# Filling whole tiles with two neighbouring columns (and no zero fill), another order of skipping, and two queues for the last stores in a sliding-window copy

## Chip, cores, metric

The kernel runs on one core of one Trainium2 chip. The metric is the device time of one execution in microseconds (us). Every ratio to the kernel before uses runs of the same rounds on the same chip. Differences to the changed kernel ("than after") compare medians of different rounds, some on other chips; the kernel before stood at 194.77 to 194.96 us in all of them, so differences of 0.2 us mean nothing.

## The reference

The input `x` is 16 x 64 x 64 x 64 float32 (batch, channels, rows, columns). The output holds each 8 x 8 window at stride 4, so 15 x 15 windows per image.

```python
n_h = (h - window_size) // stride + 1          # 15
n_w = (w - window_size) // stride + 1          # 15
for i in range(n_h):
    for j in range(n_w):
        h_start = i * stride
        w_start = j * stride
        result[:, i, j] = x[:, :, h_start:h_start + window_size, w_start:w_start + window_size].copy()
```

There is no arithmetic. 16.8 MB come in, 59.0 MB go out, and one window of one image (64 x 8 x 8 floats) is a contiguous row of 16 KB of the output.

## The kernel before

The input is loaded whole into a tile `L`. Its partition is (channel half, batch, quarter of the image's rows), so a partition holds 32 channels and 16 image rows. The loads of batch half `y=0` are issued before those of `y=1`.

A window row of the output needs all 64 channels on one partition. ScalarE (`act`) and VectorE (`dve`) therefore gather it into one of four 2 MB tiles `G`. GpSimd then stores the tile with an indirect DMA (a scatter) that sends each partition's 16 KB to the output row named by an index; an index beyond the end makes it skip that row.

```python
# (cut) idx: row of the output for partition p; adding FAR makes the scatter skip the partition
def scatter(g, ix, j, s):
    st = nc.gpsimd.indirect_dma_start(
        out=o_v, out_offset=bass.IndirectOffsetOnAxis(ap=ix[:, 0:1], axis=0),
        in_=g.rearrange("p c r w -> p (c r w)"), in_offset=None,
        element_offset=(s * NW + j) * CFREE,
        bounds_check=B * NWIN - 1, oob_is_err=False)
    free(st)

zero = ipool.tile([P, 1], f32, name="zero")
nc.vector.memset(zero[:, :], 0.0)
for g in G:
    act(out=g.rearrange("p c r w -> p (c r w)"), in_=zero.to_broadcast([P, CFREE]))

def part(y, j):                       # first phase: one batch half, so half a tile
    g = tile_()
    for half in range(CH):
        fill(g, half, half, j, y * QP, QP, (dve, dve) if y and half else (act, dve))
    scatter(g, (idx_y0, idx_y1)[y], j, 0)

def unit(j, s):
    # (cut) s == 0: a "plain" tile, 128 rows, index idx
    # s == 2: a "cross" tile; 16 of its 128 rows do not exist and are skipped:
    turn = int(crossed % 5 in (1, 3))
    crossed += 1
    fill(g, turn, s, j, 0, HP, (act, act))
    fill(g, 1 - turn, s + 1, j, 0, HP, (dve, dve))
    scatter(g, (idx_hi, idx_lo)[turn], j, s)

# (cut) order: 3 part(0, .), then 3 x (part(1, .), plain), then (cross, cross, plain) ...
# last column: two half tiles, each stored by four plain DMAs
for q in range(HQ):
    free(nc.sync.dma_start(out=o_q[q * NSLOT + s, j], in_=g_q[QP + q : QP + q + (B - 1) * HQ + 1 : HQ]))
```

A cross tile with index `idx_hi` skips its rows in the upper 64 partitions ("hi" below); one with `idx_lo` skips them in the lower 64 ("lo"). The zero fill initialises the partitions that a half tile leaves unwritten.

Of the kernel before, what the change touches and what calls it, by code (L numbers as in the profile page):

```python
# [10 lines left out]
def kernel(  # L11
# [7 lines left out]
    nc = tc.nc  # L19
    P = nc.NUM_PARTITIONS  # L20

    B, C, H, W = x.shape
    Bo, NH, NW, Co, WSo, WSo2 = out.shape
    WS = int(window_size)
    ST = int(stride)
    assert Bo == B and Co == C and WSo == WS and WSo2 == WS

    f32 = mybir.dt.float32
    i32 = mybir.dt.int32
    ALU = mybir.AluOpType  # L30
    CH = 2
    HQ = P // (B * CH)
    CL = C // CH
    RB = H // HQ
    NSLOT = RB // ST
    NWIN = NH * NW
    CFREE = C * WS * WS
    HP = P // CH
    YB = 8
    NY = B // YB  # L40
    QP = YB * HQ
# [3 lines left out]
    ipool = ctx.enter_context(tc.tile_pool(name="ipool", bufs=1))  # L45
# [3 lines left out]
    L = lpool.tile([P, CL, RB, W], f32)  # L49
# [12 lines left out]
    def itile(name):  # L62
        return ipool.tile([P, 1], i32, name=name)

    pi, tb, tq, tc_, th, idx, idx_y0, idx_y1, idx_lo, idx_hi = (
        itile(n) for n in ("pi", "tb", "tq", "tc", "th", "idx", "idx_y0", "idx_y1", "idx_lo", "idx_hi")
    )
    FAR = float(2 * B * NWIN)
    nc.gpsimd.iota(pi[:, :], pattern=[[0, 1]], base=0, channel_multiplier=1)  # L69

    def bits(d, shift, mask):
        nc.vector.tensor_scalar(out=d[:, :], in0=pi[:, :], scalar1=shift, scalar2=mask, op0=ALU.logical_shift_right, op1=ALU.bitwise_and)  # L72

    def mul(d, a, m):
        nc.vector.tensor_scalar(out=d[:, :], in0=a[:, :], scalar1=float(m), scalar2=None, op0=ALU.mult)  # L75

    def tt(d, a, b, op):
        nc.vector.tensor_tensor(out=d[:, :], in0=a[:, :], in1=b[:, :], op=op)  # L78
# [8 lines left out]
    tt(idx, tb, th, ALU.add)  # L87

    bits(th, 5, 1)
    mul(th, th, FAR)  # L90
    tt(idx_y0, idx, th, ALU.add)
    nc.vector.tensor_scalar(out=th[:, :], in0=th[:, :], scalar1=-1.0, scalar2=FAR, op0=ALU.mult, op1=ALU.add)
    tt(idx_y1, idx, th, ALU.add)

    nc.vector.tensor_scalar(out=tq[:, :], in0=tq[:, :], scalar1=float(HQ - 1), scalar2=FAR, op0=ALU.is_equal, op1=ALU.mult)
    tt(th, tc_, tq, ALU.mult)
# [17 lines left out]
    NG = 4  # L114
    G = [gpool.tile([P, C, WS, WS], f32, name=f"G{n}") for n in range(NG)]

    o_q = out.rearrange("b i j c r w -> i j b (c r w)")

    def free(st):
        tc.declare_no_dep(st.ins, group="stores", reason="each store writes rows of its own")  # L120
        tc.add_to_no_dep_group("stores", st.ins)

    def scatter(g, ix, j, s):
        st = nc.gpsimd.indirect_dma_start(  # L124
            out=o_v,
            out_offset=bass.IndirectOffsetOnAxis(ap=ix[:, 0:1], axis=0),
            in_=g.rearrange("p c r w -> p (c r w)"),
            in_offset=None,
            element_offset=(s * NW + j) * CFREE,
            bounds_check=B * NWIN - 1,  # L130
            oob_is_err=False,
        )
        free(st)

    def fill(g, half, s, j, lo, n, copies):

        d = slice(half * HP + lo, half * HP + lo + n)
        cols = slice(j * ST, j * ST + WS)
        for ch in (half, 1 - half):
            f = slice(ch * HP + lo, ch * HP + lo + n)  # L140
            cs = slice(ch * CL, (ch + 1) * CL)
            copy = copies[ch != half]
            if s < NSLOT - 1:
                copy(out=g[d, cs, :, :], in_=L[f, :, s * ST : s * ST + WS, cols])  # L144
            else:
                copy(out=g[d, cs, 0:ST, :], in_=L[f, :, s * ST : RB, cols])  # L146
                nc.vector.stream_shuffle(out=g[d, cs, ST:WS, :], in_=L[f, :, 0:ST, cols], mask=nxt)  # L147

    act, dve = nc.scalar.copy, nc.vector.tensor_copy



    EARLY = NG - 1
    zero = ipool.tile([P, 1], f32, name="zero")
    nc.vector.memset(zero[:, :], 0.0)  # L155
    for g in G:
        act(out=g.rearrange("p c r w -> p (c r w)"), in_=zero.to_broadcast([P, CFREE]))  # L157
    at = 0

    def tile_():  # L160
        nonlocal at
        at += 1
        return G[(at - 1) % NG]

    def part(y, j):
        g = tile_()
        for half in range(CH):
            fill(g, half, half, j, y * QP, QP, (dve, dve) if y and half else (act, dve))
        scatter(g, (idx_y0, idx_y1)[y], j, 0)

    crossed = 0

    def unit(j, s):
        nonlocal crossed
        g = tile_()
        if s == 0:
            for half in range(CH):
                fill(g, half, half, j, 0, HP, (act, dve))
            scatter(g, idx, j, s)
        else:  # L180

            turn = int(crossed % 5 in (1, 3))
            crossed += 1
            fill(g, turn, s, j, 0, HP, (act, act))
            fill(g, 1 - turn, s + 1, j, 0, HP, (dve, dve))
            scatter(g, (idx_hi, idx_lo)[turn], j, s)

    for j in range(EARLY):
        part(0, j)
    plain = [(j, 0) for j in range(EARLY, NW - 1)]  # L190
    cross = [(j, 2) for j in range(NW)]
    for j in range(EARLY):
        part(1, j)
        unit(*plain.pop(0))
    while plain:
        for w in cross[:2]:
            unit(*w)
        cross = cross[2:]
        unit(*plain.pop(0))


    j = NW - 1
    tile_()
    for s in range(2):
        g = tile_()
        cols = slice(j * ST, j * ST + WS)
        for y in range(NY):
            d = slice(QP + y * QP, QP + (y + 1) * QP)
            for ch, copy in enumerate((act, dve)):
                f = slice(ch * HP + y * QP, ch * HP + (y + 1) * QP)  # L210
                copy(out=g[d, ch * CL : (ch + 1) * CL, :, :], in_=L[f, :, s * ST : s * ST + WS, cols])  # L211
        g_q = g.rearrange("p c r w -> p (c r w)")
        for q in range(HQ):
            free(nc.sync.dma_start(out=o_q[q * NSLOT + s, j], in_=g_q[QP + q : QP + q + (B - 1) * HQ + 1 : HQ]))


# [33 lines left out]
```

## Time and profile before

| | before |
|---|---|
| median of its first runs | 194.92 us (194.81 to 195.02) |
| span of the profiled run | 192.9 us |
| busy: DVE, ACT, POOL | 57%, 72%, 28% |
| mean DMA rate | 393 GB/s |

The columns of a group are line, engine, operation, output<-input, count, then busy us and mean ns, then idle time before and what ended it.

```profile
DMA packets 11588, 75.81 MB, mean 393 GB/s; under 512 B 3888, under 2 KB 3888, under 8 KB 7984
...
L157 ACT COPY G<-zero 128x4096 f32<-128x4096 f32 x4 | 14.1, 3600 | 0.0
...
L157 ACT ACT_TABLE_LOAD x1 | 1.3, 1283 | 0.7 <-PEq L231 0.7
```

The table load belongs to the first ScalarE copy of the program. Here that is the zero fill, so the load runs at 0.7 us, when nobody waits for ScalarE.

### The profile page before, as it was taken

The numbers are of one execution on the slowest core, as the hardware profiler recorded it, in microseconds if no ns is written. First come the engines' busy times: TensorE is split into PE (matmuls) and PEld (weight loads), VectorE is DVE, ScalarE is ACT, GpSimd is POOL, SyncE is SP. The second block draws the span as 40 slices with busy tenths as digits, with TensorE's granted clock in tenths as the row PEclk, the third lists the DMA queues.
The fourth block names the chain that finished last, engine by engine and source line by source line (L and its number), as shares of the span: only waits on it lengthen the run. The fifth ranks groups of instructions, "written<-read, shape, count | busy, mean of one in ns | idle before, by whom it ended". The sixth has DMA issues, their size and how long they took to land.

```text
span 192.9 us, 487 instructions
## 1 busy us (share of the span) xinstructions
DVE 110.2 (57%) x153; ACT 138.3 (72%) x70; POOL 54.6 (28%) x53
## 2 busy tenths in 40 slices
DVE  5000007700999979876876875874974794723330
ACT  8993008940897879999778777877977797754560
POOL 7402212531166430422214123134043124320000
DMA  2999999999989999999999999999999999999764
GB/s 79 337 404 400 399 401 397 401 401 407 421 357 418 404 423 421 425 421 404 426 425 428 420 411 418 432 435 411 404 435 418 425 431 404 418 432 435 321 292 177
DMA packets 11588, 75.81 MB, mean 393 GB/s; under 512 B 3888, under 2 KB 3888, under 8 KB 7984
## 3 DMA queue, kind: packets, MB, share of 16 engines
q0 software_dynamic: 9472, 66.34, 83.8%
q1 hardware_dynamic: 2112, 9.44, 12.4%
q14 instruction: 4, 0.03, 0.0%
HBM read 16.78 MB, written 69.21 MB: 446 GB/s over the span
## 4 chain that ended last, share of the span: by engine, by line
DMA 73%; DVE 12%; issue 7%; POOL 2%; ACTq 1%; ACT 1%; DVEq 0%; PEldq 0%
DMA out_dram<-G,idx 34%; DMA out_dram<-G,idx_hi 22%; DMA L<-in_x_dram 16%; DVE G L144 9%; POOL L L58 2%; DVE G L146 2%; DVE G L147 2%; ACTq L245 1%; ACT G L211 1%; DVEq L144 0%; POOL pi L69 0%; DVEq L146 0%; PEldq L245 0%; ACTq L211 0%
## 5 line engine op out<-in xcount | busy, mean ns | idle before, releaser
L144 ACT COPY G<-L 64x2048 f32<-64x2048 f32 (+1 forms) x61 | 115.3, 1896 | 40.0 <-issue 20.7
L144 DVE COPY G<-L 64x2048 f32<-64x2048 f32 (+1 forms) x37 | 45.0, 1224 | 41.9 <-DMA L<-in_x_dram 27.1
L147 DVE STREAM_SHUFFLE G<-L 64x1024 f32<-64x1024 f32 x30 | 38.3, 1277 | 0.0
L146 DVE COPY G<-L 64x1024 f32<-64x1024 f32 x30 | 21.6, 720 | 21.5 <-DMA out_dram<-G,idx 16.2
L124 POOL DMA_INDIRECT out_dram<-G,idx_hi x9 | 12.0, 1338 | 34.9 <-DVE G L147 24.5
L58 POOL DMA_DIRECT2D L<-in_x_dram x16 | 11.4, 715 | 23.9 <-DMA L<-in_x_dram 23.4
L124 POOL DMA_INDIRECT out_dram<-G,idx x11 | 12.4, 1126 | 18.6 <-ACT G L144 15.9
L124 POOL DMA_INDIRECT out_dram<-G,idx_lo x6 | 8.9, 1480 | 24.1 <-DVE G L147 17.0
L124 POOL DMA_INDIRECT out_dram<-G,idx_y x6 | 9.6, 1603 | 16.0 <-ACT G L144 8.9
L157 ACT COPY G<-zero 128x4096 f32<-128x4096 f32 x4 | 14.1, 3600 | 0.0
L211 ACT COPY G<-L 32x2048 f32<-32x2048 f32 x4 | 7.6, 1896 | 7.4 <-DMA out_dram<-G,idx 4.9
L211 DVE COPY G<-L 32x2048 f32<-32x2048 f32 x4 | 4.9, 1220 | 10.1 <-DMA out_dram<-G,idx 6.6
L157 ACT ACT_TABLE_LOAD x1 | 1.3, 1283 | 0.7 <-PEq L231 0.7
L155 DVE MEMSET zero<- 128x1 f32 x1 | 0.1, 59 | 0.8 <-PEq L231 0.8
L78 DVE CUSTOM_DVE_ANT_0 idx_y<-idx,th 128x2 uint16<-128x2 uint16 x2 | 0.3, 160 | 0.1
L78 DVE TENSOR_TENSOR th<-tc,tq 128x1 int32<-128x1 int32 x2 | 0.3, 158 | 0.1
L75 DVE TENSOR_SCALAR th<-tc 128x1 int32<-128x1 int32 x2 | 0.3, 154 | 0.0
L69 POOL IOTA pi<- 128x1 int32 x1 | 0.1, 125 | 0.4 <-PEq L245 0.4
L72 DVE TENSOR_SCALAR tb<-pi 128x1 int32<-128x1 int32 x1 | 0.2, 154 | 0.1
L147 DVE LOAD_MASK_SELECT G<-L x30 | 0.2, 6 | 0.0
L78 DVE CUSTOM_DVE_ANT_0 idx_hi<-idx,th 128x2 uint16<-128x2 uint16 x1 | 0.2, 160 | 0.0
L78 DVE CUSTOM_DVE_ANT_0 idx<-tb,th 128x2 uint16<-128x2 uint16 x1 | 0.2, 159 | 0.0
(16 smaller groups left out, 2.2 us busy)
## 6 DMA issues: line engine op xcount, KB each, us to landing
L<-in_x_dram POOLq DMA_DIRECT2D x8, 1024.0 KB, 21.0
L<-in_x_dram SPq DMA_DIRECT2D x8, 896.0 KB
out_dram<-G SPq DMA_DIRECT2D x8, 256.0 KB
L<-in_x_dram POOLq DMA_DIRECT2D x8, 128.0 KB, 21.1
out_dram<-G,idx POOLq DMA_INDIRECT x11, 14.5
out_dram<-G,idx_hi POOLq DMA_INDIRECT x9, 14.1
out_dram<-G,idx_y POOLq DMA_INDIRECT x6, 9.8
out_dram<-G,idx_lo POOLq DMA_INDIRECT x6, 12.9
```

The costliest lines, as they stand in the source:

```text
L58: eng.dma_start(out=L[p0 : p0 + QP - HQ + 1 : HQ, c0:c1, :, :], in_=x_v[ch, y, q, :, c0:c1, :])
L69: nc.gpsimd.iota(pi[:, :], pattern=[[0, 1]], base=0, channel_multiplier=1)
L72: nc.vector.tensor_scalar(out=d[:, :], in0=pi[:, :], scalar1=shift, scalar2=mask, op0=ALU.logical_shift_right, op1=ALU.bitwise_and)
L75: nc.vector.tensor_scalar(out=d[:, :], in0=a[:, :], scalar1=float(m), scalar2=None, op0=ALU.mult)
L78: nc.vector.tensor_tensor(out=d[:, :], in0=a[:, :], in1=b[:, :], op=op)
L124: st = nc.gpsimd.indirect_dma_start(out=o_v, out_offset=bass.IndirectOffsetOnAxis(ap=ix[:, 0:1], axis=0), in_=g.rearrange("p c r w -> p (c ...
L144: copy(out=g[d, cs, :, :], in_=L[f, :, s * ST : s * ST + WS, cols])
L146: copy(out=g[d, cs, 0:ST, :], in_=L[f, :, s * ST : RB, cols])
L147: nc.vector.stream_shuffle(out=g[d, cs, ST:WS, :], in_=L[f, :, 0:ST, cols], mask=nxt)
L157: act(out=g.rearrange("p c r w -> p (c r w)"), in_=zero.to_broadcast([P, CFREE]))
L211: copy(out=g[d, ch * CL : (ch + 1) * CL, :, :], in_=L[f, :, s * ST : s * ST + WS, cols])
L245: with _tile.TileContext(nc) as tc:
```

## The change

The intent: the first phase should move 2 MB per scatter and not 1 MB, so that the DMA engines do not run dry between the loads and the full scatters; the skipped rows should fall evenly on the two halves; the last stores should be issued by two engines. With whole tiles no partition is left unwritten, so the zero fill goes.

```diff
-    mul(th, th, FAR)
-    tt(idx_y0, idx, th, ALU.add)
-    ... (idx_y1 = idx plus FAR for the other batch half)
+    mul(idx_y0, th, 1 - YB * NWIN)          # upper 32 of each 64: other column, same batch half
+    tt(idx_y0, idx_y0, idx, ALU.add)
+    ... (idx_y1 = idx_y0 + YB * NWIN)
-    EARLY = NG - 1
-    zero = ipool.tile([P, 1], f32, name="zero")
-    nc.vector.memset(zero[:, :], 0.0)
-    for g in G:
-        act(out=g.rearrange("p c r w -> p (c r w)"), in_=zero.to_broadcast([P, CFREE]))
+    EARLY = 3
     def part(y, j):
         g = tile_()
-        for half in range(CH):
-            fill(g, half, half, j, y * QP, QP, (dve, dve) if y and half else (act, dve))
+        for d in range(P // QP):
+            s, dj = d // NY, d % NY
+            cols = slice((j + dj) * ST, (j + dj) * ST + WS)
+            for ch in range(CH):
+                f = (ch * NY + y) * QP
+                (act if (2 * d + ch) % 3 == 0 else dve)(
+                    out=g[d * QP : (d + 1) * QP, ch * CL : (ch + 1) * CL, :, :],
+                    in_=L[f : f + QP, :, s * ST : s * ST + WS, cols],
+                )
-            turn = int(crossed % 5 in (1, 3))
+            turn = crossed % 2
-    for j in range(EARLY):
-        part(0, j)
+    for n in range(EARLY):
+        part(0, 2 * n)
 ... (cut: three cross tiles between plain ones in place of two)
-            free(nc.sync.dma_start(...))
+            free((nc.sync, nc.scalar)[s * q % 2].dma_start(...))
```

More of the change, by code (lines that the diff above doesn't have):

```diff
@@ L89 @@
     bits(th, 5, 1)
-    mul(th, th, FAR)
-    tt(idx_y0, idx, th, ALU.add)
-    nc.vector.tensor_scalar(out=th[:, :], in0=th[:, :], scalar1=-1.0, scalar2=FAR, op0=ALU.mult, op1=ALU.add)
-    tt(idx_y1, idx, th, ALU.add)
+    mul(idx_y0, th, 1 - YB * NWIN)
+    tt(idx_y0, idx_y0, idx, ALU.add)
+    nc.vector.tensor_scalar(out=idx_y1[:, :], in0=idx_y0[:, :], scalar1=float(YB * NWIN), scalar2=None, op0=ALU.add)
     nc.vector.tensor_scalar(out=tq[:, :], in0=tq[:, :], scalar1=float(HQ - 1), scalar2=FAR, op0=ALU.is_equal, op1=ALU.mult)
@@ L186, in unit @@
             scatter(g, (idx_hi, idx_lo)[turn], j, s)
-    for j in range(EARLY):
-        part(0, j)
-    plain = [(j, 0) for j in range(EARLY, NW - 1)]
+    for n in range(EARLY):
+        part(0, 2 * n)
+    plain = [(j, 0) for j in range(2 * EARLY, NW - 1)]
     cross = [(j, 2) for j in range(NW)]
-    for j in range(EARLY):
-        part(1, j)
+    for n in range(EARLY):
+        part(1, 2 * n)
         unit(*plain.pop(0))
     while plain:
-        for w in cross[:2]:
+        for w in cross[:3]:
             unit(*w)
-        cross = cross[2:]
+        cross = cross[3:]
         unit(*plain.pop(0))
@@ L213 @@
         for q in range(HQ):
-            free(nc.sync.dma_start(out=o_q[q * NSLOT + s, j], in_=g_q[QP + q : QP + q + (B - 1) * HQ + 1 : HQ]))
+            free((nc.sync, nc.scalar)[s * q % 2].dma_start(out=o_q[q * NSLOT + s, j], in_=g_q[QP + q : QP + q + (B - 1) * HQ + 1 : HQ]))
 _INS = ['x', 'window_size', 'stride']
```

## The prediction

> **What bounds the kernel now.** I read the page first (shares, slices, queues), then the table by stages, then the chain of work that ended last, then the trace's completion marks of the transfers. The page's first two parts, and its queues:
>
> ```profile
> DVE 110.2 (57%) x153; ACT 138.3 (72%) x70; POOL 54.6 (28%) x53
> ...
> DMA  2999999999989999999999999999999999999764
> ...
> q0 software_dynamic: 9472, 66.34, 83.8%
> q1 hardware_dynamic: 2112, 9.44, 12.4%
> q14 instruction: 4, 0.03, 0.0%
> ```
>
> The reader is to see that no compute engine is near full, while the DMA row is a line of nines with three weak places: the first slice, slice 12 (the 8), and the last three (764). The two data queues together fill 96% of sixteen engines' time. The table by stages (columns: stretch, its length, busy time of DVE, ACT and POOL with counts, clock, DMA share, GB/s) says how weak those places are:
>
> ```profile
> 29.50:47.90 18.40, 7.11 (x6) 10.99 (x6) 6.77 (x5) 1.00 1.06 401
> 47.90:60.00 12.10, 11.74 (x10) 11.51 (x7) 4.98 (x3) 1.00 0.92 386
> 60.00:180.00 120.00, 86.13 (x114) 96.44 (x51) 33.91 (x27) 1.00 1.01 421
> 180.00:193.00 13.00, 2.44 (x2) 3.96 (x3) 0.00 (x0) 1.00 0.60 251
> ```
>
> From 60 to 180 us the DMA engines never rest (share 1.01), so nothing that the change does to copies there can matter. Only 47.9 to 60 (0.92) and 180 to 193 (0.60) have time to win. The bytes are the same before and after: 16.8 MB in, 59.0 MB out. The trace's packets put a floor under this: a 16 KB row takes 0.618 us on one engine, a 4 KB load packet 0.163 us; 3600 x 0.618 / 16 + 4096 x 0.163 / 16 = 139.1 + 41.7 = 181 us, and the loads take about 5 us to get going. The last mark stands at 191.98 us, so about 6 us of idle engine time is spread over the later part of the run.
>
> The chain of work that ended last, its end (start, length, what):
>
> ```profile
> 139.61 42.88 DMA out_dram<-G,idx_hi x3
> 182.49 0.02 issue
> 182.51 0.02 ACTq L211
> 182.53 0.04 issue
> 182.57 1.90 ACT G L211
> 184.47 1.92 ACTq L245
> ```
>
> The second final tile (slot s=1) waits until 182.49 for a skipping scatter to land, because it needs that scatter's buffer. Then come two ScalarE copies of 1.90 us and four stores.
>
> **What the skill says, and whether the trace agrees.** (1) The Trainium skill, page "DMA: Bandwidth & Descriptors", section "The descriptor swizzle": in a 128-partition transfer partitions 0 to 63 go over engines 0 to 7 and 64 to 127 over 8 to 15. So a scatter with `idx_hi`, which skips 16 rows of the upper half, spares two rows on each of engines 8 to 15 and none on 0 to 7; `idx_lo` does the reverse. Before, 9 scatters are hi and 6 are lo. (2) Same page, section "Why a DMA increments its semaphore by 16 and not by 1": each engine posts its own completion, so the 16 marks of one scatter show how far each engine is. The trace agrees strikingly: the marks come in two groups of eight. The scatter issued at 67.51 lands at 77.80-77.91 and 78.07-79.00; that of 102.6 at 112.43-112.56 and 115.83-116.27; that of 139.61 at 148.26-148.43 and 153.47-153.77; the last one (171.71) at 180.40-180.57 and 186.56-188.52. The gap grows by about 1.3 us at each hi and falls by about 1.2 us at each lo, with some drift besides. (3) Same page, "Issuing engines are not separate DMA queues": all queues share the 16 engines; a second issuer saves issue time only. No run yet shows this here; the step below rests on it.
>
> **The change, part by part.**
>
> *Zero fill removed.* Four ScalarE copies of 3.6 us (14.1 us), done by 16.2 us; ScalarE's first real copy starts at 29.5, when loads have landed. Off the path: 0. The index arithmetic (one op of 0.15 us fewer) is done by 4.2 us, the first scatter issues at 37.2: 0.
>
> *Whole tiles in the first phase.* Before, the three scatters of the first batch half carry 64 rows each, 3 MB together, 4 rows per engine and scatter. Loads end at about 47.5; the first scatters land at 49.4-50.2, 51.9-52.6, 54.3-55.1. The next scatter, issued at 52.48, lands at 57.75-57.93 on all engines alike; four rows are 2.5 us, so it began at 55.3: the early engines idled about 0.9 us, the late group about 0.2 to 0.3 us. After, the three scatters carry 6 MB, 24 rows per engine, 15 us of work from 47.5, to 62. Is it ready in time? The instruction order shows DVE doing 2, 2, 2 and then 3, 3, 3 copies for the three tiles. Six at 1.23 us from 29.6 end at 37; nine more from 37 give tile 1 at 40.7, tile 2 at 44.4, tile 3 at 48.1. ScalarE: six at 1.90 end at 41, then 42.9, 44.8, 46.7. Plus 1 to 2 us for the issue: the first scatter queues at about 44.5, before the loads end. The fourth tile (8 copies, 5 x 1.23 = 6.2 us on DVE) is filled by 54.3, queued by 56.5, well before 62. So the dip closes. Mean gain 12.2 engine-us / 16 = 0.77 us, but the end is set by the late group, and there it is worth only **0.3 us**.
>
> *Even skipping.* Alternating gives 8 hi and 7 lo. The late group then carries two rows fewer before the last full scatter: before 4x6 + 8x10 + 8x9 + 6x6 = 212 rows, after 8x6 + 8x7 + 8x8 + 6x7 = 210. Two rows at 0.627 us (the late group's own pace, 107.85 us / 172 rows from 73.2 to 181.05) are **1.25 us**, and the early group gets two rows more than before, which it has time for. Eight against seven is as even as fifteen can be; the drift (the late group's 0.627 against 0.619) stays.
>
> *Two queues for the last transfers.* Before, SP issues the four s=1 stores at 186.41, 186.95, 187.69, 188.32, some 0.63 us apart, and a packet takes 0.62 us to drain: the engines draw as fast as SP issues. Two issuers would save at most 1.2 us of issue time, but in the late group the engines still have backlog: from the landing at 181.05 they owe 8 rows of the last scatter, 4 of s=0 and 4 of s=1, 16 x 0.627 = 10.0, to 191.1; measured: 190.87 to 191.15 for seven of them. Work, not issue, ends it: **0 to 0.2 us**.
>
> *One late engine.* The eighth mark of that group is 191.98. An 8 KB instruction fetch of the page's instruction queue falls at 181.13 and sets one engine back by over a microsecond (182.49 against 181.14 in the next scatter's marks). The fetch at 70.55 did the same, and there the lag faded from 1.1 to 0.3 us in 16 us. The fetches at 70.55 and 181.13 lie 125 VectorE instructions apart, which suggests that they are VectorE's. After, VectorE executes about 7 instructions more, so the fetch should come some 13 us earlier relative to the end and mostly fade: a guess worth 0.8 us if it fades, 0 if not; I take **0.5 us**.
>
> Sum: 0.3 + 1.25 + 0.1 + 0.5 = 2.15 us, from 194.92 to about 192.8; I choose 192.7.
>
> **Rivals.** *A. The mean counts, not the late group*: if evening out let all engines end together, the idle time of the tail (16 engines x 11.6 us less 127.6 busy, 3.6 us mean) would vanish with the dip's 0.77: 190.6, faster by 2.2%. Against it: 8 to 7 plus the drift still leaves the groups some 3 us apart, and the early group must wait for the s=1 tile anyway (buffer landing + 3.85 us copies + 1.25 us to the first packet). *B. ScalarE or VectorE becomes the bound in the first phase*: 28.5 us of ScalarE work (3 x (3 x 1.9 + 2 x 1.9)) for 30 us of DMA between 48 and 78, and the copies of the first tile could come after the loads' end. If it slipped by 3 us, a new gap of up to 3 us would eat everything: 195. For it: VectorE's first phase ends at 48.1, tight only for the third tile. Against: 4 MB are queued by then. *C. The tail is set by the s=1 chain and its issue*: then the late fetch and the second queue count in full (1.2 + 1.3 us) beside evenness: 191.3. *D. Nothing*: the fetch falls again into the last microseconds and the late group's drift grows as the early group is given more rows: 193.8.
>
> **Range and chances.** The central sum rests on two terms that I can count (0.3 and 1.25) and one that I guess (0.5). C and the upper part of A set the low end, D and a mild B the high end: 191.3 to 193.9. Faster by over 2% needs under 191.02, which only A gives: 7%. Slower by over 2% needs B far worse than I can construct: 1%.
>
> **What would show each step.** Slice 12 of the DMA row a 9 again and a share of 1.0 for 47.9 to 60: the whole tiles. The gap between the two groups of marks at the last scatter falling from 6 us to 3 or 4: even skipping. Late-group marks at about 189.5: rows. The q14 packets' times: the fetch. ScalarE's two last stores issued beside SP's but the last mark not 0.6 us or more earlier than backlog allows: the queue. The prediction is wrong if the first scatter lands after 54, if a new idle stretch opens between 48 and 80, if the groups do not close up, or if the pace per row (0.618 us) changes with two neighbouring windows per row pair.

## The result, and the profile after

The changed kernel takes 192.0 us in the median of 4 runs (191.85 to 192.54), against 194.95 us for the kernel before (4 runs). A ratio here is the mean time of one kernel's runs over that of the other's in the same rounds, so it is not quite the ratio of the medians: 0.9855, 95% interval 0.9835 to 0.9875. Executions over 1.5% slower than the fastest of the same kernel are left out of the means. The change gains 1.5%, within the 2% that is called the same, and inside the predicted range.

The page after, its shares, DMA row and queues:

```profile
DVE 120.5 (63%) x160; ACT 130.0 (68%) x69; POOL 49.9 (26%) x50
...
DMA  2999999999999999999999999999999999999974
...
DMA packets 11156, 75.81 MB, mean 399 GB/s; under 512 B 3456, under 2 KB 3456, under 8 KB 7552
...
q10 hardware_dynamic: 64, 0.52, 0.7%
```

The 8 in slice 12 has become a 9, and one of the three weak slices at the end is gone. The small packets fell by 432 = 384 + 48. The six half tiles had skipped 64 rows each, 384 in all; three scatters fewer save 3 x 16 completion marks. So a skipped row is not nothing: it leaves a 4-byte packet. The line q10 is ScalarE's queue: two stores, 0.52 MB.

The table by stages (the same columns as in the prediction):

```profile
47.90:60.00 12.10, 11.26 (x10) 11.88 (x7) 6.34 (x4) 1.00 1.01 431
60.00:180.00 120.00, 86.95 (x116) 96.70 (x52) 29.34 (x25) 1.00 1.01 422
180.00:190.10 10.10, 1.97 (x2) 3.31 (x2) 0.00 (x0) 1.00 0.64 271
```

The stretch after the loads went from a share of 0.92 and 386 GB/s to 1.01 and 431. The middle is as before: full, at 422 GB/s.

The rest is read from the completion marks, 16 per scatter, which come in two groups of eight. "Gap" is the median of the late eight less that of the early eight at the last cross scatter. "Late engine" is how much the very last mark of the run stands behind the mark before it of the same store. All times are of the profiled run.

| kernel | last cross scatter: early, late group | gap | last mark | late engine |
|---|---|---|---|---|
| before | 175.60, 181.05 | 5.45 | 191.98 | 0.83 |
| after | 175.54, 178.67 | 3.13 | 189.15 | 0.56 |

The early group is where it was. The late group is 2.4 us earlier, and the late engine costs 0.27 us less. Together that is 2.65 of the 2.83 us by which the last mark moved.

The chain of work that ended last, its end after (start, length, what):

```profile
164.83 14.61 DMA out_dram<-G,idx_hi
179.44 0.02 issue
179.46 0.02 ACTq L212
179.48 0.04 issue
179.52 1.90 ACT G L212
181.42 0.02 issue
181.44 1.90 ACT G L212
```

It has the same shape as before: the second final tile waits for a skipping scatter (179.44 us, was 182.49), then come two ScalarE copies of 1.90 us and the stores.

### The profile page after: what moved, and what is told of

It reads as the page before. It is cut to its first block, busy times and chain, and to the rows that moved or that the text cites. A ratio compares the mean times of both kernels' runs of the same rounds, so it can differ in the third digit from the quotient of the medians.

```text
span 190.1 us, 481 instructions
## 1 busy us (share of the span) xinstructions
DVE 120.5 (63%) x160; ACT 130.0 (68%) x69; POOL 49.9 (26%) x50
## 4 chain that ended last, share of the span: by engine, by line
DMA 84%; DVE 6%; ACT 3%; POOL 2%; issue 1%; ACTq 0%; DVEq 0%; PEldq 0%
DMA out_dram<-G,idx_hi 30%; DMA L<-in_x_dram 20%; DMA out_dram<-G,idx 14%; DMA out_dram<-G,idx_y 13%; DMA out_dram<-G,idx_lo 7%; DVE G L166 4%; POOL L L58 2%; ACT G L212 2%; ACT G L143 1%; DVE G L146 1%; DVE G L145 0%; DVE G L143 0%; POOL pi L69 0%; ACTq L143 0%; DVEq L145 0%
## 5 line engine op out<-in xcount | busy, mean ns | idle before, releaser
L143 ACT COPY G<-L 64x2048 f32<-64x2048 f32 x46 | 87.2, 1896 | 17.0 <-DMA out_dram<-G,idx_hi 7.6
L166 DVE COPY G<-L 32x2048 f32<-32x2048 f32 x30 | 36.9, 1230 | 28.9 <-DMA L<-in_x_dram 25.9
L166 ACT COPY G<-L 32x2048 f32<-32x2048 f32 x18 | 33.9, 1896 | 1.2 <-DMA out_dram<-G,idx_y 0.8
L145 DVE COPY G<-L 64x1024 f32<-64x1024 f32 x30 | 20.6, 688 | 16.4 <-DMA out_dram<-G,idx_hi 10.5
L143 DVE COPY G<-L 64x2048 f32<-64x2048 f32 x16 | 19.6, 1223 | 6.7 <-DMA out_dram<-G,idx 6.3
L166 ACT ACT_TABLE_LOAD x1 | 1.3, 1283 | 29.5 <-DMA L<-in_x_dram 29.5
L123 POOL DMA_INDIRECT out_dram<-G,idx_y x6 | 10.8, 1808 | 25.2 <-DVE G L166 24.1
L58 POOL DMA_DIRECT2D L<-in_x_dram x16 | 10.9, 695 | 24.1 <-DMA L<-in_x_dram 23.6
L123 POOL DMA_INDIRECT out_dram<-G,idx_hi x8 | 9.7, 1207 | 24.2 <-DVE G L146 12.3
L123 POOL DMA_INDIRECT out_dram<-G,idx_lo x7 | 8.0, 1144 | 29.4 <-DVE G L146 19.6
L123 POOL DMA_INDIRECT out_dram<-G,idx x8 | 10.2, 1270 | 18.0 <-ACT G L143 18.0
L212 ACT COPY G<-L 32x2048 f32<-32x2048 f32 x4 | 7.6, 1897 | 5.5 <-DMA out_dram<-G,idx_lo 4.5
L212 DVE COPY G<-L 32x2048 f32<-32x2048 f32 x4 | 4.9, 1220 | 8.2 <-DMA out_dram<-G,idx_lo 5.8
```

The lines of the kernel that those rows point to most:

```text
L58: eng.dma_start(out=L[p0 : p0 + QP - HQ + 1 : HQ, c0:c1, :, :], in_=x_v[ch, y, q, :, c0:c1, :])
L123: st = nc.gpsimd.indirect_dma_start(out=o_v, out_offset=bass.IndirectOffsetOnAxis(ap=ix[:, 0:1], axis=0), in_=g.rearrange("p c r w -> p (c ...
L143: copy(out=g[d, cs, :, :], in_=L[f, :, s * ST : s * ST + WS, cols])
L145: copy(out=g[d, cs, 0:ST, :], in_=L[f, :, s * ST : RB, cols])
L166: (act if (2 * d + ch) % 3 == 0 else dve)(out=g[d * QP : (d + 1) * QP, ch * CL : (ch + 1) * CL, :, :], in_=L[f : f + QP, :, s * ST : s * S ...
L212: copy(out=g[d, ch * CL : (ch + 1) * CL, :, :], in_=L[f, :, s * ST : s * ST + WS, cols])
```

## The experiments

Twelve kernels were run, all correct. The edits stand against the changed kernel, unless said otherwise. Medians of 4 to 6 runs; the kernel before ran beside them at 194.77 to 194.96 us.

| run | edit | median us | ratio to before (95% interval) |
|---|---|---|---|
| (after) | | 192.0 | 0.9855 (0.9835 to 0.9875) |
| b1_even_alone | before + even skipping | 193.8 | 0.9944 (0.9931 to 0.9957) |
| b2_whole_alone | whole tiles alone | 193.12 | 0.9917 (0.9903 to 0.9931) |
| a1_uneven | old order of skipping | 193.18 | 0.9911 (0.9895 to 0.9926) |
| a2_one_queue | one queue at the end | 191.89 | 0.9851 (0.9833 to 0.9868) |
| a3_lo_first | 7 hi, 8 lo | 190.57 | 0.9777 (0.9762 to 0.9792) |
| a4_zero_fill | zero fill put back | 190.92 | 0.9792 (0.9777 to 0.9806) |
| b3_far_columns | columns j and j+3 | 191.89 | 0.9849 (0.9836 to 0.9861) |
| b4_void | six scatters that skip all | 193.34 | 0.9924 (0.9911 to 0.9936) |
| c1_early_table | table load at the start | 189.32 | 0.9715 (0.9702 to 0.9728) |
| c3_drain | forced stop (one look) | 202.73 | (one run, state unknown) |
| c4_pad | 24 tiny VectorE fills | 191.38 | 0.9824 (0.9811 to 0.9838) |
| d1_together | table load, 7 hi 8 lo, fills | 187.79 | 0.9642 (0.9629 to 0.9655) |

### Which part gained what

**Even skipping.** One run undoes it, one has it alone on the kernel before.

```diff
-            turn = crossed % 2
+            turn = int(crossed % 5 in (1, 3))      # a1_uneven (b1_even_alone: the reverse, on the kernel before)
```

> The changed kernel with the old order of skipping (9 hi, 6 lo). Theory, rows of the late group decide the end: two more rows of 0.627 us on engines 0 to 7 before the last full scatter, so 192.0 + 1.25 = about 193.2 us, and the gap between the two groups of marks at the last cross scatter 2.5 us wider than the 3.1 us after. Rival, the tail is set by the copies and stores of the last tile and not by rows: within 0.3 us of 192.0.

> The kernel before with even skipping alone (8 hi, 7 lo). Theory: 1.25 us of rows less on the late group, 194.95 - 1.25 = 193.7 us, and the gap between the groups 2.5 us narrower than the 5.5 us before. Rival, that evenness pays only together with the whole tiles: within 0.3 us of 194.95.

Measured: 193.18 us, 1.2 us slower than after, and 193.8 us, 1.0 us faster than before. The gap at the last cross scatter is 5.50 us in the first (5.45 before) and 3.26 us in the second (3.13 after). The gap moved with the order of skipping alone, by 2.2 to 2.4 us, and the time by half of it. The times alone don't part rows from copies: the second final tile gets its buffer with the last of these marks, so its copies move along. The marks do. In the trace after, the late group's marks of the eight final stores (medians) go from 184.38 to 188.56 us, 0.60 us each, no more than a row. This group never waits for the last tile, so its rows set the end.

**Two queues.**

```diff
-            free((nc.sync, nc.scalar)[s * q % 2].dma_start(...))
+            free(nc.sync.dma_start(...))
```

> The changed kernel with all final stores issued by SyncE. Theory, the late group still has backlog when the stores of the last tile come: 0 to 0.2 us slower than 192.0. Rival, the issue of the last four stores sets the end: two issues of some 0.6 us more in a row, 1.2 us slower, about 193.2 us.

Measured: 191.89 us, the same as after. ScalarE's two stores were issued beside SyncE's (183.37 to 184.66 us in the trace after), and the last mark is 189.15 with two queues and 188.99 with one. The issue was not what ended last.

**Whole tiles.**

```diff
-            turn = crossed % 2
+            turn = int(crossed % 5 in (1, 3))
-            free((nc.sync, nc.scalar)[s * q % 2].dma_start(...))
+            free(nc.sync.dma_start(...))
```

> The changed kernel with the old order of skipping and one queue for the final stores: whole tiles alone. Theory from the two traces, first phase 1.1 us earlier for both groups (40 rows done at 72.0 in place of 73.1), and up to 0.4 us from the later-fading fetch: 193.5 to 193.9 us. Rival, the prediction's own step (only the late group's idle 0.3 us counts): 194.6 us.

Measured: 193.12 us, 1.7 us faster than before and a little better than expected. With 1.0 to 1.2 for even skipping and nothing for the queue, the parts sum to 2.7 to 2.9 us, against 2.95 measured. The table by stages shows the whole-tile kernel at a share of 1.01 after the loads, and its end as weak as before:

```profile
47.90:60.00 12.10, 11.16 (x10) 11.74 (x7) 6.36 (x4) 1.00 1.01 432
60.00:180.00 120.00, 86.34 (x115) 96.29 (x51) 30.43 (x25) 1.00 1.00 419
180.00:191.20 11.20, 2.44 (x2) 3.79 (x2) 0.00 (x0) 1.00 0.63 268
```

The marks say where the 1.7 us lie. The late group has 16 rows per engine landed at 57.25 us (57.88 before) and 40 rows at 72.05 (73.18 before). So 0.63 us come from the first 16 rows, with the idle gap in them, and 0.5 from the 24 rows after it, which took 15.30 us before and 14.80 here. The late engine lags by 0.42 and not 0.83 at the last mark: another 0.4 us.

**Are neighbouring columns part of it?** The rows after the gap might be faster because two 32-row blocks now lie side by side in memory.

```diff
-    mul(idx_y0, th, 1 - YB * NWIN)
+    mul(idx_y0, th, 3 - YB * NWIN)
-            cols = slice((j + dj) * ST, (j + dj) * ST + WS)
+            cols = slice((j + 3 * dj) * ST, (j + 3 * dj) * ST + WS)
-        part(0, 2 * n)      # and part(1, 2 * n)
+        part(0, n)          # and part(1, n)
```

> The changed kernel with columns j and j+3 paired in place of j and j+1. Theory, full tiles and no skipped rows make the first phase faster, neighbourhood in memory does not matter: 192.0 within 0.2 us, 16 KB rows still at 0.611 us between 50 and 70 us. Rival, the 0.611 us (0.62 before) comes from two windows lying side by side in memory: rows back at 0.62 there, 32 rows x 0.009 = 0.3 us or more slower.

Measured: 191.89 us, the same as after. Neighbourhood in memory makes no difference here.

**What a skipped row costs.**

```diff
+            if crossed <= 12 and crossed % 2 == 0:
+                scatter(g, idx_void, j, s)          # idx_void = idx + FAR: all 128 rows skipped
```

> The changed kernel with six more scatters in the middle that skip all their 128 rows: 48 skipped rows more per engine and 6 issues, no bytes. If a skipped row costs an engine next to nothing (the 4-byte packets show 9 ns), 48 x 0.009 = 0.4 us slower at most. If it costs some 30 ns, as the 0.7 us that the half tiles of before lost over 24 skipped rows per engine would need, 48 x 0.03 = 1.4 us slower, about 193.4 us.

Measured: 193.34 us, 1.34 us slower, close to the second figure. The marks agree: each void scatter lands some 0.18 us after the scatter ahead of it on every engine (100.11 then 100.29, 113.80 then 113.98). That is 1.1 us for six, and 0.18 / 8 = 22 ns per skipped row, its share of the completion mark included. The 24 skipped rows per engine of the kernel before would thus cost about 0.5 us in all, an estimate. Its own marks show less: its first three scatters (4 rows and 4 skips per engine) land 2.42 to 2.44 us apart, half of the 4.85 us of a whole tile after. The fourth comes 3.03 us behind the third on the late group (54.85 and 57.88), so the 0.63 us is an idle gap and not the skips. Only 8 skips fall among the 24 rows after the gap (0.18 of the 0.5 us there, at most), so the rest of that 0.5 is pace, the time per row.

### Eight to seven is not even

```diff
-            turn = crossed % 2
+            turn = 1 - crossed % 2
```

> The changed kernel with 7 hi and 8 lo. Theory, the late group is late by its slower rows and by one hi too many, so sparing it two rows still moves the end: up to 1.25 us faster, about 190.8 us, with the two groups of marks within 1 us of each other at the last cross scatter. Rival, eight to seven is as even as it gets and either order is the same, or the last tile's copies then bound: within 0.3 us of 192.0, or the other group late by as much.

Measured: 190.57 us, 1.4 us faster than after. The gap at the last cross scatter is 0.77 us (176.77 and 177.53), and the last stretch is fuller than the 0.64 after:

```profile
180.00:188.90 8.90, 0.83 (x1) 2.35 (x2) 0.00 (x0) 1.00 0.75 309
```

So "even" in the change's sense was not even for the engines. The late group is also late by slower rows, and giving it the larger share of the skips is worth as much again as the change's own step.

### The zero fill that was not free to remove

```diff
     EARLY = 3
+    zero = ipool.tile([P, 1], f32, name="zero")
+    nc.vector.memset(zero[:, :], 0.0)
+    for g in G:
+        act(out=g.rearrange("p c r w -> p (c r w)"), in_=zero.to_broadcast([P, CFREE]))
```

> The changed kernel with the zero fill of all four buffers put back. Theory, it ends at 16 us, 13 us before the first copy can start, so 0: 192.0 within 0.2 us. Rival, the fill slows the loads by its writes or its extra instructions: 0.5 us or more slower and loads landing later than 47.9 us.

Measured: 190.92 us, 1.1 us **faster** than after. Both theories were wrong. The timelines show the trail. After (start, length, engine, line, operation, count, idle time before and its end):

```profile
29.52 1.28 ACT L166 ACT_TABLE_LOAD   x1 [29.52 <-DMA L<-in_x_dram]
```

```profile
44.49 1.38 POOL L123 DMA_INDIRECT out_dram<-G,idx_y  x1 [8.49 <-DVE G L166]
```

With the zero fill put back:

```profile
29.55 17.00 ACT L170 COPY G<-L 32x2048 f32<-32x2048 f32 x9 [13.40 <-issue]
...
43.25 1.42 POOL L123 DMA_INDIRECT out_dram<-G,idx_y  x1 [7.20 <-ACT G L170]
```

Without the zero fill, the table load stands at 29.52 us, after the wait for the input and right ahead of the first copy. ScalarE starts 1.3 us later, and the first scatter is issued at 44.49 and not 43.25 us. The Trainium skill, page "ScalarE: Activation LUTs", section "What ACT_TABLE_LOAD costs", gives about 1283 ns for the load; this trace has 1283 ns too.

Yet the engines are at work on loads until about 47 us in both, and the first scatter lands at the same time (medians 52.32 and 52.54 after, 52.25 and 52.67 with the fill). What differs is the pace from there on. So I put the load alone at the start:

```diff
     EARLY = 3
+    zero = ipool.tile([P, 1], f32, name="zero")
+    nc.vector.memset(zero[:, :], 0.0)
+    warm = ipool.tile([P, 1], f32, name="warm")
+    act(out=warm[:, :], in_=zero[:, :])
```

> The changed kernel with one tiny ScalarE copy (one element per partition) at the start, so that the table load of 1.28 us runs at 1 us and not at 29.5 us, just ahead of the first fill; no zero fill. The zero fill put back gave 190.92 us against 192.0, with the first scatter issued at 43.25 and not 44.49 us. If that gain came through the table load (the first scatter is queued before the first engines finish their loads at 46.4 us, so that they do not start their rows together): about 190.9 us, and whole scatters landing 4.86 us apart up to 92 us. If it came from the fill itself: 192.0 as before.

Measured: 189.32 us, 2.7 us faster than after, well beyond what was expected. Its timelines:

```profile
0.74 1.28 ACT L154 ACT_TABLE_LOAD   x1 [0.74 <-PEq L236]
...
29.56 16.98 ACT L170 COPY G<-L 32x2048 f32<-32x2048 f32 x9 [27.34 <-DMA L<-in_x_dram]
```

```profile
43.24 1.42 POOL L123 DMA_INDIRECT out_dram<-G,idx_y  x1 [7.21 <-ACT G L170]
```

The rate in the full middle, by the table of stages, 80 to 160 us. Before:

```profile
80.00:160.00 80.00, 59.71 (x82) 66.45 (x36) 21.98 (x18) 1.00 1.00 420
```

After:

```profile
80.00:160.00 80.00, 60.28 (x89) 65.80 (x35) 20.23 (x17) 1.00 1.01 421
```

With the table load at the start:

```profile
80.00:160.00 80.00, 61.88 (x90) 67.32 (x36) 20.81 (x18) 1.00 1.01 431
```

The DMA share is 1.00 to 1.01 in all three: the engines never rest. Yet 431 GB/s flow in place of 421. A full DMA row is thus not the engines' peak. In the packets, a 16 KB row begun between 100 and 110 us takes 0.625 us in the mean before and after and 0.612 with the early load.

What sets the pace? In the four kernels whose first scatter was issued by 43.3 us (a4, c1, c3, d1), whole scatters of the first phase land 4.84 to 4.91 us apart up to at least 80 us. In the eight with whole tiles and an issue at 44.2 us or later they stretch to 4.9 us and more from 70 to 80 us on. The 16 marks of the third scatter lie spread over 0.81 to 1.10 us in the four, and over 0.42 to 0.72 in seven of the eight (0.94 in c4_pad, where one late engine stands apart). A row takes 0.61 us, so in the first set the engines start their rows spread over the whole time of a row, in the second more in bunches. To test whether being bunched is the cause, the next run starts from the good pace and bunches the engines on purpose.

```diff
+        if n == 1:                                   # about 72 us; with the zero fill kept
+            for a, b in ((3, 0), (0, 1), (1, 2), (2, 3), (3, 0), (3, 1), (3, 2)):
+                dve(out=G[b][:, 0:C:CL, 0:WS:ST, 0], in_=G[a][:, 0:C:CL, 0:WS:ST, 0])
```

> The changed kernel with the zero fill kept, and at about 72 us a forced stop: seven tiny VectorE copies that touch all four buffers, so that all stores must land before the next tile is filled, and all 16 engines restart together from rest. It is slow by some 10 us on purpose; only the pace is read. With the zero fill and without the stop, whole scatters land 4.86 us apart between 52 and 92 us. Theory, engines that start their 16 KB rows together get in each other's way: 5.0 to 5.1 us for the first whole scatters after the restart, and 4.9 or more after, as in the kernel before after its gap at 55 us. Rival, the pace hangs on something else (time, the copies that run beside): 4.86 us again.

Measured by its profile (one run, 202.73 us, state unknown, slow on purpose), by stages ahead of and behind the stop:

```profile
50.00:72.00 22.00, 15.43 (x13) 16.98 (x9) 7.87 (x5) 1.00 1.00 429
93.00:120.00 27.00, 22.01 (x34) 23.84 (x14) 7.05 (x7) 1.00 1.00 418
120.00:180.00 60.00, 45.62 (x65) 50.25 (x27) 15.44 (x13) 1.00 1.01 421
```

The zero-fill kernel without the stop, over the same times:

```profile
93.00:120.00 27.00, 19.98 (x31) 22.67 (x13) 7.01 (x7) 1.00 1.01 426
120.00:180.00 60.00, 40.53 (x56) 46.10 (x25) 12.81 (x11) 1.00 1.00 421
```

Ahead of the stop whole scatters land 4.84 us apart (76.27, 81.11). After it all 16 marks of the first scatter lie within 0.13 us. The next whole scatter takes 4.96 us, a later one 4.97: slower, though less than the 5.0 to 5.1 expected. So right after the restart from rest 418 GB/s flow, where the same kernel without the stop has 426. The 421 from 120 us on is not the stop's work, for without it that kernel gets there too. The kernel before looks the same: its marks at 57.75 to 57.93 us, after its gap, lie within 0.18 us, and a half tile takes 2.53 us from there on in place of 2.42 to 2.44. So with a gap of half a microsecond it lost the idle time, and the good pace as well.

The spread of all 16 marks can't be the whole answer: in the trace after it grows to 2 us and more with the gap between the groups, and the pace stays slow. The spread within a group of eight fits better. In the zero-fill run the whole scatter issued at 131.63 us took 4.87 us on the early group, whose marks lie 0.59 us apart, and 5.00 us on the late group, whose marks lie within 0.28 us: the same kernel at the same time, beside the same copies. In the trace after, the early group's marks of that stage lie within 0.20 us and it took 4.94. That bunched engines are slower is thus likely and not shown: there is one stop in one run, and it changed more than the bunching.

What stays open: how 1.25 us of earlier issue spread the starts was not shown. That the first engines run out of loads before the scatter's rows reach them fits the packets (the loads end between 46.4 and 47.9 us), but no run delayed single engines. Also open is why the zero-fill kernel loses part of the good pace after 100 us (425 GB/s between 80 and 160 us) while the early-load kernel mostly keeps it (428 GB/s from 120 to 180 us). The fill moves the table load just as far, and gained 1.1 us where the early load gained 2.7. And which shared part of the chip bunched engines contend for, no run tells.

### The late engine

```diff
     EARLY = 3
+    pad = ipool.tile([P, 1], f32, name="pad")
+    for _ in range(24):
+        nc.vector.memset(pad[:, :], 0.0)
```

> The changed kernel with 24 tiny VectorE fills at the start, where VectorE idles. If the instruction fetches at 62.5 and 165.0 us are VectorE's [...], they come 24 instructions earlier: the first before 50 us, within the loads, the second near 145 us, and the late engine's lag at the end falls from 0.56 us to 0.2 or less: 0.3 to 0.5 us faster, 191.5 to 191.7 us. If the pace between 62 and 92 us was upset by the first fetch too, up to 1 us more. Rival, the fetches belong to another engine: both stay where they are, 192.0 us.

Measured: 191.38 us, 0.6 us faster. The four 8 KB fetches of the trace stood at 62.46, 105.72, 112.04 and 164.97 us after. Here they stand at 38.68, 105.69, 111.91 and 147.18: the first and the last moved, so these two are VectorE's. The late engine's lag in the last mark fell from 0.56 to 0.02 us. The rows slowed at about the same time as after although the first fetch had gone, so that fetch is not what upsets the pace.

The Trainium skill, page "Runtime: NRT & Kernel Launch", section "Instruction fetch mechanics", says that instructions are refilled in blocks of 16 KiB and that this is mostly hidden. This trace shows packets of 8 KB, 125 VectorE instructions apart before. VectorE did not wait for them, but one store engine, presumably the one that carried the fetch, fell up to 1.3 us behind its group (166.33 against 165.07 us after, in the first marks behind the fetch at 164.97).

### Together

> The changed kernel with three of the tried edits together: table load at the start (189.32 us alone), 7 hi and 8 lo (190.57 alone), 24 tiny VectorE fills at the start (191.38 alone). The gains do not add: with rows at 0.611 us the late group is only 1.8 us late at the last hi scatter, so lo first is worth about half of a two-row swing, 0.5 to 0.6 us, and the moved fetch the late engine's 0.35 us. Expected 189.3 - 0.9 = 188.4 us, between 188.0 and 188.9. If the three added in full (2.7 + 1.4 + 0.6 from 192.0) it would be 187.3 us; if the pads or the other order upset the spread of the engines' starts, 189.3 or more with rows at 0.618 us.

Measured: 187.79 us, 0.9642 of the kernel before, better than the expected range: my estimate was 0.2 us or more too cautious at its low end. The rate stays at 430 GB/s, the gap at the last cross scatter is 0.86 us, the late engine lags 0.14 us:

```profile
60.00:180.00 120.00, 89.00 (x117) 100.22 (x53) 33.21 (x25) 1.00 1.01 430
180.00:186.10 6.10, 0.00 (x0) 0.00 (x0) 0.00 (x0) 1.00 0.64 269
```

What I had missed is probably idle time ahead of the stores of the second final tile. Its buffer came free at 175.41 us, against 176.76 with the early load alone, where one late engine held it back by 0.58 us. From 178 to 183 us the DMA share is 1.01 here and was 0.88 there. No run parted this from the rest. This version beats both kernels.

## Why the prediction was right

The forecast of 192.7 us (191.3 to 193.9) stands against 192.0. Its steps, one by one:

- **What bounds: right.** From 60 to 180 us the share is 1.01 after, as before; the bytes are the same; the change's gains came from the late group and the ends. But the step from there, that nothing done to copies can matter in a full stretch, is wrong: with the table load moved, 431 GB/s flow there in place of 421. The floor of 181 us is not fixed either: it takes the medians of the packets' times, and the means of the same packets (0.624 and 0.168 us) give 183, so less was idle than the 6 us that it leaves.
- **Even skipping, 1.25 us: right.** 1.2 us by undoing it, 1.0 by adding it alone, and the gap between the groups moved by 2.2 to 2.4 us, nearly as two rows plus two rows should.
- **Two queues, 0 to 0.2 us: right.** 0 within noise; work, not issue, ended last.
- **Whole tiles, 0.3 us: the step that was mis-sized.** In its place the marks show 0.63 us of idle gap on the late group and 0.5 us of slower rows after it, together 1.1 us. The working took the wait from 2.5 us per four rows (measured: 2.42 to 2.44) and the last mark of the group, and looked no further than the gap. A slower pace after the gap was not in the sum; the forced stop shows one in a single run.
- **The late engine, 0.5 us: right in kind, about half in size.** Its lag in the last mark fell from 0.83 to 0.56 us. The fetch came 16 us earlier, at 164.97 us (13 were guessed), but the lag faded only partly in the time left. That the fetch is VectorE's was argued then and is shown by the pads.
- **Zero fill removed, 0: wrong.** The step looked at the copies and not at the table load that they brought early. Once they were gone the load ran just ahead of the first fill and delayed the first scatter's issue by 1.25 us. Nothing waited for that, since the loads were still running; what changed was the pace later on. Putting the fill back gained 1.1 us, putting the load alone at the start 2.7 us. With the load moved, the same change reaches 189.3 us.
- **"As even as fifteen can be": wrong.** 7 hi and 8 lo gained 1.4 us. Counting rows evenly is not timing them evenly; the drift, which I had left standing, was the reason to choose the other order.

Of the rivals, A (all idle time vanishes), B (ScalarE or VectorE bound in the first phase), C (the s=1 chain and its issue) and D (nothing gained) did not come about. B was nearest to something real: the first scatter did come later than it could, and with this went pace rather than a gap.

The sum came out near for a reason that is partly luck: the whole tiles gave 0.8 us more than written, the late engine 0.2 less, and the measured figure of the whole tiles holds a loss through the table load that the prediction did not know of.

## What to carry to other kernels

When DMA engines are full, read the completion marks of each transfer: groups that drift apart show whose work sets the end, and an uneven split of skips or rows can be chosen to bring them together. Before removing a copy that looks off the path, see what else it brought early, such as an engine's table load. Also, a full DMA row is not a fixed rate: here it carried 421 or 431 GB/s, 2% apart, and was slower after a forced stop. That the spread of the engines' starts makes the difference fits the traces and is not shown.

## What the Trainium skill lacked or had wrong

- "DMA: Bandwidth & Descriptors": no word that engines which are always busy with the same kind of stores can run at two rates. Here 421 and 431 GB/s at a share of 1.00 to 1.01 (80 to 160 us), and 4.84 against 4.96 us per whole scatter ahead of and behind a forced stop.
- The same page: no cost for rows that an indirect scatter skips. Here each leaves a 4-byte packet, and in scatters of nothing but skipped rows costs about 22 ns on its engine; six such scatters cost 1.34 us.
- "Runtime: NRT & Kernel Launch" says that instruction refills come in 16 KiB blocks and are mostly hidden. Here they are 8 KB packets, one per 125 to 132 VectorE instructions. They were hidden from VectorE, but the page has nothing on what they do to other transfers: after VectorE's one store engine falls up to 1.3 us behind, and moving the two gained 0.6 us.
- "ScalarE: Activation LUTs" has the table load's 1283 ns right, and says that the load stands right before the operation that needs it. It doesn't say what follows when that operation waits for data: here the load ran only after the wait, at 29.52 us. A tiny copy at the start moves it to 0.74 us, which gained 2.7 us.
